# The sample attention's cache rows on SyncE's queue, loaded ahead as one stream

## The chip, the core and the metric

The kernel runs on one core of one Trainium2 chip. The metric is device time in microseconds of one execution. Three runs of the kernel before took 2106.47 to 2107.64 us, median 2107.42 us. One further execution was profiled; its trace spans 2100.4 us from the first to the last instruction.

Engine names are those of the profile: PE (TensorE's matrix products) and PEld (its weight loads), DVE (VectorE), ACT (ScalarE), POOL (GpSimd), and SP (SyncE), which here does nothing but issue DMAs. All DMAs, whoever issues them, are carried by the core's 16 DMA engines. L1062 is line 1062 of the kernel that the row belongs to.

## The reference, cut to what matters

One decoder layer runs for 256 prompt tokens and for 8 sample sequences of 4 tokens each (288 columns together). The part that the change touches is the sample tokens' attention over cached keys and values, in three groups of heads with different strides:

```python
DIL_GROUPS = ((128, 1), (512, 4), (2048, 16))

def _dilated_group(q, k, v, q_idx, dil, n_back):
    dist = jnp.arange(n_back + 1) * dil
    idx = q_idx[:, None] - dist[None, :]
    valid = idx >= 0
    idx = jnp.maximum(idx, 0)
    kg = k[:, idx].astype(jnp.float32)
    vg = v[:, idx].astype(jnp.float32)
    s = jnp.einsum('bqhd,bqjhd->bqhj', q.astype(jnp.float32), kg) * (HD_B ** -0.5)
    s = jnp.where(valid[None, :, None, :], s, -jnp.inf)
    m = jnp.max(s, axis=-1)
    p = jnp.exp(s - m[..., None])
    return jnp.einsum('bqhj,bqjhd->bqhd', p, vg), m, jnp.sum(p, axis=-1)
...
    h = _rms_norm(x, g_pre_mix)
    (qa, ka, va, za, ba, aa, qb, kb, vb, uc, ga, gb, gc) = _split(h @ w_in, IN_SPLITS)
...
    kv_all = [jnp.concatenate([win_hists[gi].astype(dt), kv_new[gi]], axis=1) for gi in range(N_GROUPS)]
```

Beside it stand a gated delta rule, a pooling branch, the prompt's own attention, a merge, and a feed-forward block. All weights are float32, 2048 wide, and each is read once.

## The kernel before, in words

**The weight stream.** Every projection is a list of weight tiles `raw` of 256 rows by 512 columns (512 KB). `load` issues the tile's DMA on SyncE's queue into one of five buffers. `feed` splits it: ACT casts it to `wh` (L180), and DVE subtracts to get the remainder `wl` (L184); each has three buffers. PE then runs 24 matmuls of 128x288 for the tile (L229 to L231): `wh` with the high part of the activations, `wh` with the low part, `wl` with the high part. A tile's third matmul therefore waits for DVE.

**Background work.** After each tile `step` advances a few generators by a rate. `attn_sample` is one of them: about 3.65 of its steps per tile, one DVE instruction each. The order of all instructions on an engine is fixed when the kernel is built, by a scheduler with a simulated timeline, and each engine executes its own in that order.

**The sample attention.** Two passes over 59 rows each, first over the keys, then over the values. A *row* is a tile `kr` of 128 partitions by 512 numbers (256 KB). In each pass, in this order: 32 rows of group 1 and 16 rows of group 2 from the caches `cache_win2` and `cache_win3` (L1062), two rows of this step's own keys or values, each loaded by four DMAs of 64 KB from a DRAM scratch `scr` (L1043), eight rows of group 0 from `cache_win1` (L1071), and one more from the scratch (L1074). A row of groups 1 and 2 is used by four DVE instructions, one per head; a row of group 0 by sixteen. In the first pass they write `junk` and a score (L1083), in the second they accumulate into `ot` or `big` (L1130, L1132). Between the passes come the maxima and exponentials. Each DVE instruction of the passes waits for the one before it (`chain`).

**Where a row's 128 partitions come from.** For groups 1 and 2 the cached tokens are taken apart as `(q m r)`, and one row takes four neighbouring tokens `r` of each of 32 blocks:

```python
src = cw[g].rearrange("b (q m r) k h d -> m k r (b q) (h d)", q=4, r=dil)
dq.dma_start(kr, src[m, kv][:4])
```

So the DMA's source is 4 by 32 by 512 numbers, outermost size 4, with 2 KB in one piece. Rows of group 0 have a source of 128 by 512, as the weight tiles have 128 outermost.

**Queues.** `dq` is GpSimd's queue. On it stand, in the scheduler's order, the row loads, POOL's own arithmetic for the delta rule and the pooling branch, and stores of states and of new keys and values (`win_prompt`, `scr`, `win_sample`, `gdn_prompt`, `gdn_sample`). There are five `kr` buffers; a load waits until DVE has used up the row that was in its buffer, and whatever stands behind it on POOL waits too. On SyncE's queue stand the weight tiles, the delta rule's states and small transposes, and later copies of the caches.

Of the kernel before, what the change touches and what calls it, by code (L numbers as in the profile page):

```python
# [9 lines left out]
F32 = mybir.dt.float32  # L10
# [4 lines left out]
PSUM = bass.MemoryType.PSUM  # L15
DRAM = bass.MemoryType.DRAM
# [6 lines left out]
TAIL = 'eveqqqeeeqqqevqe'  # L23
PM_POOL = (5, 7, 9, 11, 13, 15)
PCB = 3
SQP = (1, 3, 5, 7, 9, 11, 13)
EPS = 1e-6
SC = 128.0 ** -0.5
# [61 lines left out]
class Layer:  # L90
# [3 lines left out]
    def __init__(self, ctx, tc, a, o):  # L94
        self.ctx, self.tc, self.nc, self.a, self.o = ctx, tc, tc.nc, a, o
        P = self.pool
        self.cp = P("cp")
        self.raw_p = P("rawp", 5)
        self.wh_p = P("whp", 3)
        self.wl_p = P("wlp", 3)  # L100
        self.up = P("up")
        self.sm = P("sm", 2)
        self.dr = P("dr", space=DRAM)
        self.pm = P("pm", 4, space=PSUM)
        self.pb = P("pb", 4, space=PSUM)
        self.ufree = deque(range(NU))
        self.uslot = {}
        self.bg = []
        self.chained = {}
        self.tiles = deque()  # L110
        self.pend = deque()
        self.items = []
        self.n = 0
        self.raws = deque()
        self.hold = None
        self.out_a, self.out_b, self.out_c = {}, {}, {}
        self.dq = self.nc.gpsimd
# [1 line left out]
    def pool(self, name, bufs=1, **k):  # L119
        return self.ctx.enter_context(self.tc.tile_pool(name=name, bufs=bufs, **k))  # L120

# [1 line left out]
    def U(self, cols=NT, dt=F32, name="u"):  # L123
        s = self.ufree.popleft()
        self.n += 1
# [28 lines left out]
            off += w  # L154
        return d

# [1 line left out]
    def load(self):  # L158
        nc, parts = self.nc, self.tiles.popleft()
        left = len(self.tiles)  # L160
# [81 lines left out]
        return ins  # L242

    def chain(self, ins, key="sample"):
        """Each of these instructions waits for the one before: what the projections need gets between them."""
        if key in self.chained:
            self.behind(ins, self.chained[key])
        self.chained[key] = ins
# [18 lines left out]
        self.bg.append(g)  # L267
        return g

# [1 line left out]
    def cache_copies(self):  # L271
        """Chunks of the window caches' kept rows, copied in DRAM between the weight tiles."""
        for g in (2, 1, 0):
            keep = (124, 508, 1024)[g]
            src, dst = self.a[f"cache_win{g + 1}"][0], self.o[f"win{g + 1}_sample"][0]
            r0 = src.shape[1] - keep
            step = (124, 127, 128)[g]
            for b in range(8):
                for r in range(0, keep, step):
                    yield dst[b, r:r + step], src[b, r0 + r:r0 + r + step]  # L280
# [33 lines left out]
        self.free(t)  # L314

    def warm_sqrt(self, src):
        """Has the square root's table loaded ahead of its use."""
        self.nc.scalar.activation(self.small(1, "warm"), src[:, 0:1], AF.Sqrt)

    def rms_rows(self, *accs):  # L320
        """1 / rms of the tokens, along the free dimension of all partitions (in PSUM)."""
        nc, st = self.nc, (0, 128, 160)
        p = self.ps("rms")
        for k, acc in enumerate(accs):
            for i, t in enumerate(st):
                nc.tensor.matmul(p[:, i:i + 1], lhsT=acc[:, t:t + 128], rhs=self.c["ones"][:, 0:1],
                                 start=k == i == 0, stop=k == len(accs) - 1, skip_group_check=True)
        r = self.small(3, "rs")
        nc.scalar.activation(r, p[:, 0:3], AF.Sqrt, bias=self.eps, scale=1.0 / D)
        nc.vector.reciprocal(r, r)  # L330
        p = self.ps("rmsb")
        for i, t in enumerate(st):
            nc.tensor.transpose(p[:, t:t + 128], r[:, i:i + 1].to_broadcast([128, 128]), self.c["ident"])
        return p[:, :NT]
# [11 lines left out]
            self.xT.append(x)  # L346

    def pre_norm(self, n):
        """x times the gain, split: the first projections run on it, and their outputs take the rows' rms."""
        for d in range(len(self.h0), n):  # L350
            self.h0.append(self.scaled_split(self.xT[d], self.p["g_pre_mix"][:, d:d + 1], "h0"))

# [110 lines left out]
            nc.scalar.activation(t2, pe[:, hg * 32:hg * 32 + 32], AF.Exp)  # L463
            self.egls.append(t2)

# [1 line left out]
    def mixer_plan(self):  # L467
        w = self.a["w_in"][0]
        H = lambda: self.h
# [76 lines left out]
        self.nc.gpsimd.dma_start(self.o["cstate"], self.cstate.rearrange("p a b -> p (a b)"))  # L546
        self.pa.__exit__(None, None, None)

# [1 line left out]
    def gdn_setup(self):  # L550
        nc, p = self.nc, self.pap
        self.pads = []
# [62 lines left out]
    def gdn(self, hg):  # L615
# [36 lines left out]
        for x in X9:  # L652
# [17 lines left out]
            if x < 8:  # L670
                t = self.U(name="lt4")
# [7 lines left out]
        nc.sync.dma_start(dlt.rearrange("x p i -> p x i"), ltc)  # L679
        lb = pp.tile([32, 32, 32], F32, name="lb")  # L680
        nc.sync.dma_start(lb.rearrange("p j i -> p (j i)"), dlt.rearrange("x (b j) i -> (x b) (j i)", b=4))
        # sample tokens
        for _ in self.gdn_sample(hg, G, LA[8], kn[4], bv[4], beta, egc, nbe, kdc, qsc):
            yield
        self.free(LA.pop(8), kn.pop(), bv.pop(), G["kqs"])
# [121 lines left out]
    def gdn_sample(self, hg, G, la, kn, bv, beta, egc, nbe, kdc, qsc):  # L807
# [55 lines left out]
        nc.vector.tensor_tensor(so, so, qsc[:, X:X + 1], op=OP.mult)  # L863
        nc.scalar.activation(o[:, 0:128], o[:, 0:128], AF.Copy, scale=so)
        yield
        # state update: block (l, b) of the masked outer products
        kd = kn[:, 0:128]
        nc.gpsimd.tensor_scalar(kd, kd, kdc[:, X:X + 1], None, op0=OP.mult)
        vz = [self.U(name="vz") for _ in range(4)]
# [35 lines left out]
        G["os"] = o  # L905
        yield

# [1 line left out]
    def evac_qkv(self, kind, g):  # L909
        vT = []  # L910

        def evac(h, ps):
            nc = self.nc
            t = self.res.popleft()
            nc.scalar.copy(t, ps)
            if kind == 2:
                vT.append(t)
            else:
                (self.kT if kind == 1 else self.qT)[g, h] = t
            if h < 3:  # L920
                return
            src = vT if kind == 2 else [(self.kT if kind == 1 else self.qT)[g, j] for j in range(4)]
            for tb in ([2] if kind == 0 else [1, 2] if (kind == 1 and g == 0) else [0, 1, 2]):
                w = NS if tb == 2 else 128
                p = self.ps("knat")
                for j in range(4):
                    nc.tensor.transpose(p[:w, j * 128:j * 128 + 128], src[j][:, tb * 128:tb * 128 + w],
                                        self.c["ident"])
                for hp in range(2):
                    n = self.U(name="nat")  # L930
                    cs = slice(hp * 256, hp * 256 + 256)
                    if hp == 0:
                        nc.scalar.copy(n[:w, :256], p[:w, cs])
                    else:
                        nc.vector.tensor_copy(n[:w, :256], p[:w, cs])
                    if tb < 2:
                        if not (g == 0 and tb == 0):
                            o = self.o[f"win{g + 1}_prompt"][0, 0].rearrange("r k h d -> r k (h d)")
                            r0 = 0 if g == 0 else tb * 128
                            self.dq.dma_start(o[r0:r0 + 128, kind - 1, cs], n[:, :256])  # L940
                    else:
                        self.dq.dma_start(self.scr[kind, g][:, cs], n[:NS, :256])
                        if kind > 0:
                            o = self.o[f"win{g + 1}_sample"][0].rearrange("b r k h d -> b r k (h d)")
                            self.dq.dma_start(o[:, WIN[g] - 4:, kind - 1, cs], n[:NS, :256])
                    if kind == 2 and tb < 2:
                        self.vn[g, tb, hp] = n
                    else:
                        self.free(n)
            self.free(*vT)  # L950
        evac.res = 4
        return evac

# [77 lines left out]
    def attn_sample(self, pool):  # L1031
# [8 lines left out]
        def by_t(dst, kind, g):  # L1040
            src = scr[kind, g].rearrange("(b t) d -> t b d", t=4)
            for t in range(4):
                dq.dma_start(dst[t * 32:t * 32 + 32], src[t][:, None, :].to_broadcast([8, 4, 512]))  # L1043
# [7 lines left out]

        cw = [a["cache_win1"][0], a["cache_win2"][0], a["cache_win3"][0]]

        def row():
            return pool.tile([128, 512], F32, name="kr", bufs=5)

        def rows(kv):
            for g, dil, n in ((1, 4, 32), (2, 16, 16)):
                src = cw[g].rearrange("b (q m r) k h d -> m k r (b q) (h d)", q=4, r=dil)
                for m in range(n):  # L1060
                    kr = row()
                    dq.dma_start(kr, src[m, kv][:4])  # L1062
                    yield g, (m if g == 1 else 32 + m), kr
            for g in (1, 2):
                kr = row()
                by_t(kr, 1 + kv, g)
                yield g, 47 + g, kr
            src = cw[0].rearrange("b (s m) k h d -> m k (b s) (h d)", m=8)
            for m in range(8):
                kr = row()  # L1070
                dq.dma_start(kr, src[m, kv])  # L1071
                yield 0, m, kr
            kr = row()
            dq.dma_start(kr, scr[1 + kv, 0][:, None, :].to_broadcast([32, 4, 512]))  # L1074
            yield 0, 8, kr

        for g, m, kr in rows(0):
            for h in range(4):
# [75 lines left out]
            nc.vector.tensor_copy(self.ob[h][:, NP:], p[:, h * 32:h * 32 + 32])  # L1154
        yield

# [1 line left out]
    def pool_open(self):  # L1158
        self.drain(self.attn_p)
        self.pc = self.tc.tile_pool(name="pc", bufs=PCB, side="right", reuse_waits="tile")  # L1160
# [66 lines left out]
        for k in range(4):  # L1227
            self.free(*self.pooled[gp * 4 + k])

# [1 line left out]
    def evac_gate(self, n):  # L1231
        def evac(b, ps):
            t = self.res.popleft()
# [89 lines left out]
        nc.scalar.copy(self.r2, self.rms_rows(acc))  # L1323
        self.free(acc)

# [1 line left out]
    def evac_ffn_gate(self, f):  # L1327
        def evac(b, ps):
            self.drain(self.ffn_rms)
# [134 lines left out]
```

## Time and profile before

| what | us |
|---|---|
| runs (three) | 2106.47 to 2107.64, median 2107.42 |
| span of the profiled execution | 2100.4 |
| DVE busy in the span | 1320.4 |
| ACT busy | 886.4 |
| POOL busy | 340.2 |
| rows used in the first pass, from the first to the last start (L1083) | 419.9 to 666.3 |
| rows used in the second pass (L1130, L1132) | 688.4 to 974.6 |

The profile's page gives a total for the profiled execution only as its span; 2107.42 less 2100.4 leaves 7.0 us that lie around the span. Times within the trace are counted from the span's start. A view by windows gives, for a stretch of time, each engine's busy time with its number of instructions, then the mean granted TensorE clock (1.00 is full), the mean busy share of the 16 DMA engines, and GB/s. The DMA share can exceed 1, since packets on one engine overlap a little. In the DMA view a queue's share is the time that its packets took, as a share of 16 engines over the stretch; q1 is SyncE's queue and q0 GpSimd's.

### The profile page before, as it was taken

Reading aid. Unit: us, or ns where it says so; the run is one execution under the profiler, and the core shown is the slowest. Engines: PE = TensorE matmul, PEld = TensorE weight load, DVE = VectorE, ACT = ScalarE, POOL = GpSimd, SP = SyncE. Lnnn points to the kernel's source line nnn. Section 1 sums busy time; section 2 is a strip of 40 time slices with the busy share of each in tenths; the row PEclk is TensorE's granted clock in tenths of the full one; section 3 lists DMA queues with packets and bytes.
Section 4 is the critical chain, followed back from the end, with each engine's and each line's share of the span. In section 5 each row is a group of like instructions: output and inputs, shape, how many; then the busy total and the mean of one; then the engine's idle time right before and its main releaser. Section 6 shows DMA issues by size and latency. Waiting matters only on the chain. (4 is left out here: it accounts for less than half of the span.)

```text
span 2100.4 us, 38731 instructions
## 1 busy us (share of the span) xinstructions
PE 2026.7 (96%) x15218; PEld 1996.9 (95%) x15218; DVE 1320.4 (63%) x2829; ACT 886.4 (42%) x1402; POOL 340.2 (16%) x570
## 2 busy tenths in 40 slices
PE   8999899989899998999999989999999999999998
PEld 7999798979899898999999989999999999999997
DVE  7979557577787788997347475543455445544455
ACT  4654374343354333433334453343334333333344
POOL 4426403543311222201000030000000000000001
PEclk9999999999999999999999999999999999999999
DMA  6565446899965899765577746767776767776762
GB/s 233 156 192 180 132 145 190 215 210 235 235 184 157 190 215 232 222 186 161 161 257 225 224 142 221 225 218 229 224 229 213 227 215 226 221 228 217 225 208 97
DMA packets 229048, 425.50 MB, mean 203 GB/s; under 512 B 42738, under 2 KB 66818, under 8 KB 227202
## 3 DMA queue, kind: packets, MB, share of 16 engines
q1 hardware_dynamic: 194912, 380.52, 60.8%
q0 software_dynamic: 33808, 41.92, 8.3%
q8 instruction: 119, 1.95, 0.4%
q10 hardware_dynamic: 144, 0.59, 0.1%
q14 instruction: 65, 0.52, 0.1%
HBM read 410.44 MB, written 66.63 MB: 227 GB/s over the span
## 5 line engine op out<-in xcount | busy, mean ns | idle before, releaser
L184 DVE TENSOR_TENSOR wl<-raw,wh 128x1024 fp32r<-128x1024 f32 x585 | 721.5, 1234 | 545.0 <-ACT wh L180 541.3
L180 ACT CAST wh<-raw 128x1024 fp32r<-128x1024 f32 x585 | 612.6, 1049 | 923.0 <-PE m L230 842.3
L229 PE MATMUL m<-hh,wh 128*128 128x288 f32 x1792 | 537.3, 302 | 10.2 <-DVE xp L1175 5.5
L231 PE MATMUL m<-hh,wl 128*128 128x288 f32 x1792 | 527.6, 300 | 13.5 <-DVE wl L184 13.5
L230 PE MATMUL m<-hl,wh 128*128 128x288 f32 x1792 | 534.0, 299 | 0.0
L229 PE MATMUL m<-xgh,wh 128*128 128x288 f32 x1408 | 414.7, 296 | 3.4 <-DVE fg L1331 1.8
L231 PE MATMUL m<-xgh,wl 128*128 128x288 f32 x1408 | 414.8, 296 | 2.5 <-DVE wl L184 2.5
L230 PE MATMUL m<-xgl,wh 128*128 128x288 f32 x1408 | 415.5, 296 | 1.0 <-DVE xgl L339 0.9
L231 PEld LDWEIGHTS m<-hh,wl 128*128 128x128 f32 x1792 | 338.5, 191 | 17.9 <-DVE wl L184 15.9
L229 PEld LDWEIGHTS m<-hh,wh 128*128 128x128 f32 x1792 | 341.7, 191 | 14.5 <-DVE xp L1175 6.0
L230 PEld LDWEIGHTS m<-hl,wh 128*128 128x128 f32 x1792 | 341.9, 191 | 1.3 <-issue 1.2
L229 PEld LDWEIGHTS m<-xgh,wh 128*128 128x128 f32 x1408 | 265.5, 189 | 4.3 <-DVE fg L1331 2.3
L230 PEld LDWEIGHTS m<-xgl,wh 128*128 128x128 f32 x1408 | 266.6, 189 | 2.1 <-DVE xgl L339 2.0
L231 PEld LDWEIGHTS m<-xgh,wl 128*128 128x128 f32 x1408 | 265.5, 189 | 3.0 <-DVE wl L184 3.0
L230 PE MATMUL m<-hidl,wh 128*128 128x288 f32 x704 | 207.5, 295 | 0.0
L229 PE MATMUL m<-hidh,wh 128*128 128x288 f32 x704 | 207.1, 294 | 0.0
L231 PE MATMUL m<-hidh,wl 128*128 128x288 f32 x704 | 206.5, 295 | 0.0
L1392 POOL TENSOR_TENSOR yo<-y,xr 128x288 f32<-128x288 f32 x7 | 5.6, 829 | 828.9 <-DVE y L1383 828.9
L230 PEld LDWEIGHTS m<-hidl,wh 128*128 128x128 f32 x704 | 132.4, 188 | 0.0
L229 PEld LDWEIGHTS m<-hidh,wh 128*128 128x128 f32 x704 | 132.2, 188 | 0.0
L231 PEld LDWEIGHTS m<-hidh,wl 128*128 128x128 f32 x704 | 132.1, 188 | 0.0
L1062 POOL DMA_DIRECT2D kr<-cache_win x96 | 65.6, 685 | 198.3 <-DVE junk L1083 80.1
(389 smaller groups left out, 2766.0 us busy)
## 6 DMA issues: line engine op xcount, KB each, us to landing
raw<-w_in SPq DMA_DIRECT2D x247, 512.0 KB, 4.3
raw<-w_gu SPq DMA_DIRECT2D x176, 512.0 KB, 4.0
raw<-w_down SPq DMA_DIRECT2D x88, 512.0 KB, 5.0
win_sample<-cache_win SPq DMA_DIRECT2D x64, 512.0 KB, 5.3
kr<-cache_win POOLq DMA_DIRECT2D x112, 256.0 KB, 10.6
raw<-w_out SPq DMA_DIRECT2D x32, 512.0 KB, 4.5
win_sample<-cache_win SPq DMA_DIRECT2D x32, 508.0 KB, 5.4
st<-state_gdn SPq DMA_DIRECT2D x64, 128.0 KB, 3.2
```

What stands on the lines that cost most here:

```text
L180: i = nc.scalar.copy(wh, raw)
L184: self.last_wl = nc.vector.tensor_tensor(wl, raw, wh.bitcast(F32), op=OP.subtract)
L229: nc.tensor.matmul(out, lhsT=wh[:, kk, c], rhs=xh, start=k == 0, stop=False)
L230: nc.tensor.matmul(out, lhsT=wh[:, kk, c], rhs=xl, start=False, stop=False)
L231: nc.tensor.matmul(out, lhsT=wl[:, kk, c], rhs=xh, start=False, stop=k == 2 * nk - 1)
L1062: dq.dma_start(kr, src[m, kv][:4])
L1392: (nc.vector if how == "v" else nc.gpsimd).tensor_tensor(out[:, d % 2], y, x, op=OP.add)
```

## The change

The rows of both passes become one list. A generator `ahead` keeps up to six rows loaded or under way and hands out the oldest; a row is handed out when the passes ask for it, so five more are on their way at that moment. The loads go out on SyncE's queue, and there are six `kr` buffers. A row that comes from the scratch still takes four DMAs where it did. `self.values` holds back the loads of the second list's later groups until the last value projection has been written to the scratch. What is computed, and the DVE instructions of the passes, stay as they were.

```diff
+KR = 6
...
+        self.values = False
...
             self.free(*vT)
+            self.values = self.values or (kind == 2 and g == 2)
...
-        def row():
-            return pool.tile([128, 512], F32, name="kr", bufs=5)
-
-        def rows(kv):
+        sq = nc.sync
+
+        def load(src, cached):
+            kr = pool.tile([128, 512], F32, name="kr", bufs=KR)
+            if cached:
+                sq.dma_start(kr, src)
+            else:
+                for t in range(4):
+                    sq.dma_start(kr[t * 32:t * 32 + 32], src[t][:, None, :].to_broadcast([8, 4, 512]))
+            return kr
+
+        def sources(kv):
+
             for g, dil, n in ((1, 4, 32), (2, 16, 16)):
                 src = cw[g].rearrange("b (q m r) k h d -> m k r (b q) (h d)", q=4, r=dil)
                 for m in range(n):
-                    kr = row()
-                    dq.dma_start(kr, src[m, kv][:4])
-                    yield g, (m if g == 1 else 32 + m), kr
+                    yield g, (m if g == 1 else 32 + m), src[m, kv][:4], True
             for g in (1, 2):
-                kr = row()
-                by_t(kr, 1 + kv, g)
-                yield g, 47 + g, kr
+                yield g, 47 + g, scr[1 + kv, g].rearrange("(b t) d -> t b d", t=4), False
             src = cw[0].rearrange("b (s m) k h d -> m k (b s) (h d)", m=8)
             for m in range(8):
-                kr = row()
-                dq.dma_start(kr, src[m, kv])
-                yield 0, m, kr
-            kr = row()
-            dq.dma_start(kr, scr[1 + kv, 0][:, None, :].to_broadcast([32, 4, 512]))
-            yield 0, 8, kr
+                yield 0, m, src[m, kv], True
+            yield 0, 8, scr[1 + kv, 0][:, None, :].to_broadcast([32, 4, 512]), True
+
+        def ahead():
+
+            todo = deque((kv,) + r for kv in range(2) for r in sources(kv))
+            got = deque()
+            while todo or got:
+                while todo and len(got) < KR:
+                    if todo[0][0] and not self.values:
+                        break
+                    kv, g, m, src, cached = todo.popleft()
+                    got.append((kv, g, m, load(src, cached)))
+                yield got.popleft()
+
+        stream = ahead()
+
+        def rows(kv):
+            for _ in range(59):
+                r = next(stream)
+                assert r[0] == kv
+                yield r[1:]
```

How this moves instructions on two engines, in the order in which each engine executes them. First SyncE's queue, from the delta rule's last small transpose (`dc`) on, where the first pass begins. Before:

```order
L704 DMA dc<-dx_4950 128x8x32 x2
L169 DMA raw<-w_in 128x2x512 x48
L169 DMA raw<-w_br_a 128x2x512 x4
L169 DMA raw<-w_in 128x2x512 x8
L169 DMA raw<-w_br_a 128x2x512 x4
```

And with the change, at the same place (its lines stand up to two lower in the file):

```order
L706 DMA dc<-dx_4950 128x8x32 x2
L171 DMA raw<-w_in 128x2x512 x4
L1062 DMA kr<-cache_win 128x1x512 x6
L171 DMA raw<-w_in 128x2x512 x3
L1062 DMA kr<-cache_win 128x1x512 x2
L171 DMA raw<-w_in 128x2x512
L1062 DMA kr<-cache_win 128x1x512 x2
L171 DMA raw<-w_in 128x2x512
L1062 DMA kr<-cache_win 128x1x512
L171 DMA raw<-w_in 128x2x512
```

The row loads now stand between the weight tiles' loads, first six in a row and then one or two behind each tile, in both passes.

Then GpSimd, at the same place of the program: the queries' loads (`qt`, `big`), the delta rule's arithmetic (`e`, `la`) and stores (`scr`, `win_prompt`, `win_sample`, `gdn_prompt`). Before:

```order
L1049 DMA big<-scr 128x1x512 x4
L1062 DMA kr<-cache_win 128x1x512 x5
L714 TENSOR_TENSOR e_539_5137<-la_4057,cc 128x128
L942 DMA scr<-nat_5038 32x256
L942 DMA scr<-nat_5041 32x256
L1062 DMA kr<-cache_win 128x1x512
L721 TENSOR_TENSOR la_4057<-la_4057,cc 128x128
L1062 DMA kr<-cache_win 128x1x512
L1043 DMA qt<-scr 32x1x512 x4
L1062 DMA kr<-cache_win 128x1x512 x11
L940 DMA win_prompt<-nat_5459 128x256
```

And with the change:

```order
L1052 DMA big<-scr 128x1x512 x4
L716 TENSOR_TENSOR e_539_5137<-la_4057,cc 128x128
L944 DMA scr<-nat_5038 32x256
L944 DMA scr<-nat_5041 32x256
L723 TENSOR_TENSOR la_4057<-la_4057,cc 128x128
L1046 DMA qt<-scr 32x1x512 x4
L942 DMA win_prompt<-nat_5459 128x256
```

GpSimd's rows are the same without the row loads. On PE, ACT and DVE the change moves a few neighbours past each other, mostly DVE's row instructions against its `wl`, and takes away or adds none.

## The prediction

> **What bounds the kernel now.** I read the page's busy shares first, then the windows of the two stretches in which row loads are dense, then who waits there, then the DMA view.
>
> ```profile
> span 2100.4 us, 38731 instructions
> PE 2026.7 (96%) x15218; PEld 1996.9 (95%) x15218; DVE 1320.4 (63%) x2829; ACT 886.4 (42%) x1402; POOL 340.2 (16%) x570
> ```
>
> PE is busy for all but 74 us, so only PE's idle time and its slow clock can be won, while anything that keeps weight tiles from it costs in full. The windows say where the change acts:
>
> ```profile
> core 0: us, PE busy (x) PEld busy (x) DVE busy (x) ACT busy (x) POOL busy (x), PEclk, DMA share, GB/s
> 410.00:560.00 150.00, 130.87 (x952) 128.17 (x950) 99.93 (x456) 57.79 (x114) 55.20 (x90) 0.95 0.99 221
> 700.00:850.00 150.00, 138.44 (x1000) 136.24 (x1000) 121.79 (x278) 53.16 (x70) 38.93 (x76) 0.97 1.03 222
> 1000.00:1050.00 50.00, 50.00 (x380) 50.00 (x380) 20.40 (x18) 19.67 (x24) 0.00 (x0) 1.00 0.55 160
> ```
>
> The first two are the stretches of groups 1 and 2, call them A (keys) and B (values). PE idles 19.1 us in A and 11.6 us in B, and the clock is below 1, while after the attention (1000 to 1050) PE never idles. The DMA engines are full in A and B (0.99, 1.03) at 221 and 222 GB/s. DVE's and PE's waits from 400 to 880 us (us in total, times, longest):
>
> ```profile
> DVE junk L1083 <- DMA kr<-cache_win: 43.8, 17, 8.5
> DVE ot L1132 <- DMA kr<-cache_win: 22.9, 15, 5.0
> PE m L231 <- DVE wl L184: 14.0, 7, 5.8
> ```
>
> The longest gap, in the timeline (start, duration, and the idle time before with what ended it), DVE first:
>
> ```profile
> 555.43 0.08 DVE L1083 DVE_READ_ACCUMULATOR junk<-kr,qt 128x1 f32 x1
> 560.12 0.29 DVE L1083 SCALAR_TENSOR_TENSOR junk<-kr,qt 128x128 f32<-128x128 f32 x1 [4.61 <-DMA kr<-cache_win]
> 560.34 1.22 DVE L184 TENSOR_TENSOR wl<-raw,wh 128x1024 fp32r<-128x1024 f32 x1
> ...
> 561.62 0.61 PE L231 MATMUL m<-hh,wl 128*128 128x288 f32 x1 [5.80 <-DVE wl L184]
> ```
>
> DVE stands 4.61 us before a late row, the remainder `wl` stands behind that row in DVE's fixed order, and PE waits 5.80 us for `wl`. Late rows are what stops PE. The question is what makes a row late, the issue on GpSimd or the transfer, and whether SyncE's queue changes that.
>
> **What GpSimd's queue costs.** Groups and waits of the tile `kr` in A (the second line: time that POOL's later loads stood for a row before):
>
> ```profile
> L1062 POOL DMA_DIRECT2D kr<-cache_win x44: 677/679/716, 412.7 to 546.4; - x44
> POOL kr L1062 <- DVE junk L1083: 43.3, 19, 7.5
> DMA to landing us min/median/max: 5.9/10.6/15.6
> ```
>
> A load occupies POOL 0.68 us (44 of them 30 us of 150) and mostly waits for a buffer that DVE empties: the scheduler already runs loads ahead as far as five buffers allow. Moving them frees POOL, which bounds nothing here (55.20 us busy in A), and the sixth buffer adds one row of lead. A row lands 10.6 us after its issue, so the transfer is what is slow.
>
> **What a row is to the DMA engines.** Between the passes there is a moment with one row load and nothing else: the window, and the same moment's queue line (packets, MB, share of 16 engines).
>
> ```profile
> 691.70:694.70 3.00, 3.00 (x24) 2.81 (x23) 2.88 (x7) 2.53 (x4) 0.00 (x0) 1.00 0.24 75
> q0 software_dynamic: 78, 0.23, 24.5%
> ```
>
> 24.5% of 16 is four: a row with a source of outermost size 4 uses 4 of the 16 DMA engines, 64 KB (65.5 thousand bytes) each, at 75 / (0.24 x 16) = 19.5 GB/s per engine. Now A and B in full (queue lines, then issues with their count and size):
>
> ```profile
> q1 hardware_dynamic: 8643, 16.66, 49.1%
> q0 software_dynamic: 15110, 16.31, 49.0%
> ...
> raw<-w_in SPq DMA_DIRECT2D x31, 512.0 KB, 9.9
> kr<-cache_win POOLq DMA_DIRECT2D x44, 256.0 KB, 9.9
> ```
>
> ```profile
> q1 hardware_dynamic: 11779, 21.66, 65.4%
> q0 software_dynamic: 11295, 11.42, 36.9%
> ...
> raw<-w_in SPq DMA_DIRECT2D x32, 512.0 KB, 11.6
> kr<-cache_win POOLq DMA_DIRECT2D x40, 256.0 KB, 12.6
> raw<-w_br_a SPq DMA_DIRECT2D x5, 512.0 KB, 10.6
> raw<-w_pool SPq DMA_DIRECT2D x4, 256.0 KB, 4.5
> ```
>
> In A GpSimd's queue fills 49.0% of the engines, twice what four can. So different rows on that queue sit on different fours, and the load spreads over all sixteen. No load on SyncE's queue before has an outermost size below 16, so no row shows which four it would use there. That is the open point on which everything hangs.
>
> **The sum if SyncE's queue always takes the same four** (my forecast). Then those four carry every row, plus a sixteenth of all else (32.8 thousand bytes per weight tile). At 19.5 GB/s a row takes 65.5 / 19.5 = 3.36 us and a tile 1.68 us on each of them.
> - A: 44 rows 147.8; 31 tiles 52.1; the rest of q0, 16.31 less 44 x 0.262 = 4.78 MB, over 16 engines, 15.3. Together 215 in place of 150 us: +65.
> - B: 40 rows 134.4; 32 + 5 + 4 half tiles = 39 tiles 65.5; 0.93 MB 3.0. Together 203: +53.
> - Slack: five tiles of lead can be used up in each stretch (8.4 us) and the sixth buffer brings one row (3.36): -24 for both. The 12 rows of groups 1 and 2 outside the stretches are loaded where DMA has room, as before.
> - POOL's freed issues and the DVE order: 0. They lie beside a longer wait; without that cover they are the gain of the first rival.
>
> Sum: +94 on the profiled execution, 2100.4 span and 7.0 around it, so 2107.4 + 94 = 2201; the execution stands at the median of the runs by that count. I say **2200**.
>
> The per-engine rate is the unknown price. Its ends: the weights alone in one microsecond, 356 / (0.95 x 16) = 23.4, and A itself, 221 / (0.99 x 16) = 14.0.
>
> ```profile
> 1010.00:1011.00 1.00, 1.00 (x10) 1.00 (x9) 0.86 (x1) 0.10 (x1) 0.00 (x0) 1.00 0.95 356
> ```
>
> At 23.4 A takes 179, B 169, less 20 of slack: +28, 2135. At 14.0 they take 300 and 283, less 33: +250, 2357. I take the row load alone, since four busy engines are that case, and lean below the top because weights mix in. So this case has its own range, 2135 to 2320.
>
> The Trainium skill, "DMA: Bandwidth & Descriptors", section "Why a DMA increments its semaphore by 16 and not by 1", says that a DMA runs on the largest count up to 16 that divides the outermost sizes of both sides, on the sync queue on the lowest-numbered engines, on GpSimd's on consecutive ones from a moving cursor. The trace agrees with the count (24.5%) and with the moving (49.0%); no run here shows SyncE's side. By that rule this case holds.
>
> **Rivals.**
> - *SyncE's queue spreads the rows.* The engines share the load as now. What can be won is PE's idle time in A and B, 19.1 + 11.6, and the slow clock, 0.05 x 150 + 0.03 x 150 = 12: at most 43 us, to 2064. For it: POOL's issue is gone, and one more row leads. Against: the engines are already full at 221 GB/s, so at the same rate the same bytes take the same time. Half of the bound: 2086.
> - *Spread, and nothing changes.* If 221 GB/s is what this mix of reads gives, the rows are as late as before, less one row of lead. 2107. The same page, section "Issuing engines are not separate DMA queues", says that queues share the 16 engines and that another issuer saves only issue time; by that the sum would be 0.
> - *Spread, but SyncE blocks.* A row load waits for its buffer until DVE has used a row, and weight tiles now stand behind it on SyncE; they wait themselves for a buffer that `wl` frees. With five tiles of lead this decides only when the row load waits longer than about four tiles, 4 x 24 / 7.6 = 12.6 us (380 matmuls in 50 us). DVE's longest wait of 8.5 us is below it; two such waits in one stretch would cost some 5 us each: 2117. Behind SyncE's waiting load also stands `poolh`, on which the pooling branch waits.
>
> That the change does not do what it says is excluded by the order: the loads stand on SyncE's queue, six ahead.
>
> **Chances.** Same four 0.70: SyncE's weight loads all cover the sixteen alike, nothing in the trace shows its queue moving on from one load to the next, and a load cut in four most plainly starts where all start. Spread and faster 0.16; spread and the same 0.09; blocking 0.05. The likeliest time is 2200. The range takes the first case from the cheap end to 2300 and, on the other side, the same, the blocking and the weaker part of the gain: 2090 to 2300. A measurement of this kernel can tell about 0.2% (4 us) from no change: slower 0.75, same 0.09, faster 0.16.
>
> **What would show it.** Right: in A and B of the new trace a DMA share well below 1 with landings of rows and tiles longer than now; DVE waiting on `kr` far above 67 us in total, PE on `wl`; a stretch of only row loads showing a share of about 0.25 however many are under way; POOL without row waits. Wrong: a DMA share near 1 in A and B, or shorter landings of `kr`; then the rows are spread, and the time falls or stays. If the four are fixed but the sum is off, the per-engine rate in A (GB/s over sixteen times the share) says by how much.

## The result, and the profile after

| kernel | median us | runs | ratio to before (95% interval) |
|---|---|---|---|
| before | 2106.94 | 2101.92 to 2107.64 (4) | |
| with the change | 2180.31 | 2178.31 to 2184.15 (4) | 1.0362 (1.0344 to 1.0380) |

The change makes the kernel 73.4 us slower. The profiled execution took 2178.31 us. Its page, in the lines that answer to those of before, begins with the span and the busy time of each engine:

```profile
span 2176.5 us, 38746 instructions
PE 2056.5 (94%) x15218; PEld 2020.6 (93%) x15218; DVE 1320.5 (61%) x2829; ACT 884.4 (41%) x1402; POOL 256.9 (12%) x440
```

The span grew by 76.1 us. PE runs the same 15218 matmuls in 29.8 us more (2056.5 against 2026.7), which goes with a lower granted clock (0.971 against 0.984 on the mean), and idles 46.3 us more (120.0 of the span against 73.7). DVE's and ACT's work is unchanged, and POOL has 83 us less of it. In the page's 40 slices of 54 us PE's holes stand from the eighth to the eleventh and from the fifteenth to the seventeenth, where the rows of groups 1 and 2 are loaded, with the DMA engines half to three quarters busy there:

```profile
PE   8998999878799977899999998999999999999998
DMA  7566356755575555665557774766676777767663
```

The rows of groups 1 and 2 now take longer to be used up. In the view of the tile `kr` the first pass (durations min/median/max in ns, then the first and the last start in us) reads, before and then after:

```profile
L1083 DVE SCALAR_TENSOR_TENSOR junk<-kr,qt x200: 253/291/296, 419.9 to 568.4; 128x128 f32<-128x128 f32 x100
```

```profile
L1107 DVE SCALAR_TENSOR_TENSOR junk<-kr,qt x200: 268/291/296, 411.8 to 609.0; 128x128 f32<-128x128 f32 x100
L1154 DVE TENSOR_SCALAR ot<-kr,sct x4: 275/279/285, 726.1 to 729.1; 128x128 f32<-128x128 f32 x4
L1156 DVE SCALAR_TENSOR_TENSOR ot<-kr,sct,ot x196: 334/352/405, 730.3 to 944.8; 128x128 f32<-128x128 f32 x196
```

So the keys' stretch, from the first to the last use, went from 148.5 to 197.2 us, and the values' (726.1 to 944.8) from 182.1 (688.4 to 870.5 before) to 218.7: +49 and +37. The windows of the two stretches, with the columns that the prediction's first table has:

```profile
410.00:600.00 190.00, 147.37 (x918) 140.86 (x917) 101.87 (x467) 51.54 (x104) 20.61 (x38) 0.85 0.54 166
760.00:930.00 170.00, 137.40 (x903) 133.17 (x902) 109.21 (x248) 44.97 (x57) 12.12 (x31) 0.89 0.60 180
```

Where the DMA engines were full before (0.99 at 221 GB/s), they now look half idle (0.54 at 166 GB/s), and yet everything waits for them. PE idles 42.6 us of the first stretch at a clock of 0.85. The waits from 400 to 960 us say for what (us in total, times, longest):

```profile
ACT wh L182 <- DMA raw<-w_in: 139.6, 34, 14.5
...
DVE junk L1107 <- DMA kr<-cache_win: 75.3, 38, 4.1
DVE wl L186 <- ACT wh L182: 60.9, 37, 6.4
...
PE m L233 <- DVE wl L186: 19.4, 16, 3.5
DVE ot L1156 <- DMA kr<-cache_win: 17.9, 13, 3.8
```

DVE waits 93 us for rows in place of 67. The largest wait is new in its size: ACT waits 139.6 us for weight tiles, where it waited 10.3 us before. Both kinds of load are late now.

The key to it is a moment in which little but rows is under way, here from 488 to 501 us: first the window, then the queue and the issues in it.

```profile
488.00:501.00 13.00, 8.01 (x56) 7.78 (x55) 5.75 (x30) 5.74 (x13) 0.33 (x1) 0.84 0.27 100
```

```profile
q1 hardware_dynamic: 632, 1.25, 25.5%
...
kr<-cache_win SPq DMA_DIRECT2D x5, 256.0 KB
```

Five row loads are issued in those 13 us, and SyncE's queue still keeps 25.5% of the sixteen engines busy, which is four. On GpSimd's queue the same kind of load had filled 49.0% before. SyncE's own timeline at this place (start, duration of the issues):

```profile
481.45 2.78 SPq L171 DMA_DIRECT2D raw<-w_in  x1
484.32 13.34 SPq L1062 DMA_DIRECT2D kr<-cache_win  x6
500.16 2.36 SPq L171 DMA_DIRECT2D raw<-w_in  x1
```

For some 16 us, from the end of one weight tile's issue to the start of the next, SyncE issues nothing but rows, and its six issues take 13.34 us of it. In the stretch from 420 to 600 us a weight tile's issue takes 2.9 us in the median, against 0.37 us before:

```profile
L169 SPq DMA_DIRECT2D raw<-w_in x41: 367/368/368, 421.4 to 592.7; - x41
```

```profile
L171 SPq DMA_DIRECT2D raw<-w_in x28: 391/2872/4729, 418.9 to 592.1; - x28
L1062 SPq DMA_DIRECT2D kr<-cache_win x42: 546/1372/4571, 423.4 to 583.9; - x42
```

Three theories can explain this much.

- **Theory 1, the same four engines.** Every row of groups 1 and 2 goes to the same four engines on SyncE's queue. Those four are the bound, and SyncE's slow issues follow from it: the four are behind, and the queue takes no more.
- **Theory 2, SyncE's order.** Rows and tiles share one in-order queue; a row load that waits for its buffer holds up the tiles behind it. How many engines a row uses does not matter.
- **Theory 3, the pieces.** A row is 128 pieces of 2 KB from far-apart addresses, which is slow to issue or to fetch on SyncE's queue, whatever engines carry it.

### The profile page after: what moved, and what is told of

It is laid out like the page before. It is cut to its first block, busy times and chain, and to the rows that moved or that the text cites. A ratio compares the mean times of both kernels' runs of the same rounds, so it can differ in the third digit from the quotient of the medians.

```text
span 2176.5 us, 38746 instructions
## 1 busy us (share of the span) xinstructions
PE 2056.5 (94%) x15218; PEld 2020.6 (93%) x15218; DVE 1320.5 (61%) x2829; ACT 884.4 (41%) x1402; POOL 256.9 (12%) x440
## 5 line engine op out<-in xcount | busy, mean ns | idle before, releaser
L231 PE MATMUL m<-hh,wh 128*128 128x288 f32 x1792 | 547.1, 307 | 22.9 <-DVE xp L1199 9.9
L233 PE MATMUL m<-hh,wl 128*128 128x288 f32 x1792 | 537.1, 306 | 19.1 <-DVE wl L186 18.9
L232 PE MATMUL m<-hl,wh 128*128 128x288 f32 x1792 | 543.0, 304 | 0.0
L231 PEld LDWEIGHTS m<-hh,wh 128*128 128x128 f32 x1792 | 350.3, 196 | 28.2 <-DVE xp L1199 10.3
L233 PEld LDWEIGHTS m<-hh,wl 128*128 128x128 f32 x1792 | 346.4, 195 | 26.2 <-DVE wl L186 24.2
L232 PEld LDWEIGHTS m<-hl,wh 128*128 128x128 f32 x1792 | 350.5, 196 | 1.3 <-issue 1.2
L1107 DVE SCALAR_TENSOR_TENSOR junk<-kr,qt 128x128 f32<-128x128 f32 x200 | 57.8, 289 | 87.9 <-DMA kr<-cache_win 75.3
```

Source lines behind the costliest of these rows:

```text
L231: nc.tensor.matmul(out, lhsT=wh[:, kk, c], rhs=xh, start=k == 0, stop=False)
L232: nc.tensor.matmul(out, lhsT=wh[:, kk, c], rhs=xl, start=False, stop=False)
L233: nc.tensor.matmul(out, lhsT=wl[:, kk, c], rhs=xh, start=False, stop=k == 2 * nk - 1)
L1107: self.chain(nc.vector.scalar_tensor_tensor(junk, kr[:, hs], SC, q, op0=OP.mult, op1=OP.mult, accum_out=out))
```

## The experiments

The first three keep the change and its instructions, in the same order on every engine, and alter only the source's outermost size. Ratios are to runs of the kernel before beside them: 2104.74 us median of 8 for the first four experiments, 2104.68 us of 7 for the others.

**32 outermost.** The same pieces and bytes per row, with the 32 blocks ahead of the 4 neighbours:

```diff
-                src = cw[g].rearrange("b (q m r) k h d -> m k r (b q) (h d)", q=4, r=dil)
+                src = cw[g].rearrange("b (q m r) k h d -> m k (b q) r (h d)", q=4, r=dil)
-                    yield g, (m if g == 1 else 32 + m), src[m, kv][:4], True
+                    yield g, (m if g == 1 else 32 + m), src[m, kv][:, :4], True
```

> Only the order of a row's 128 source pieces is changed (32 blocks outermost, 4 tokens inside), so a row's partitions stand in another order than the queries and the sample scores belong to other tokens; every instruction stands where it stands in the changed kernel, and the same bytes are read in the same 2 KB pieces. Theory 1 (the four engines): a row now spreads over 16 engines, the hot four are gone, 2065 to 2110, likeliest 2090. Theory 2 (SyncE's order: weight tiles stand behind row loads that wait for a buffer): order and waits are the same, 2180 as the changed kernel. Theory 3 (making a row's 128 pieces costs SyncE 1 to 3 us each): as many pieces, 2180.

Measured: 2052.47 us (2050.84 to 2060.28, 4 runs), ratio 0.9738 (0.9697 to 0.9778). Windows of the stretches that the prediction calls A and B, and the issue of a row, which took up to 8.45 us with the change:

```profile
410.00:560.00 150.00, 148.15 (x1143) 147.10 (x1142) 126.17 (x566) 67.41 (x129) 29.20 (x54) 1.00 0.87 272
700.00:850.00 150.00, 148.45 (x1116) 147.68 (x1115) 137.21 (x309) 61.04 (x79) 14.90 (x32) 1.00 0.73 233
...
L1062 SPq DMA_DIRECT2D kr<-cache_win x112: 328/540/1357, 406.7 to 849.5; - x112
```

PE is busy for 148 of 150 us at full clock, and 272 GB/s move at a share of 0.87. SyncE's order is untouched, and the pieces are the same but for their order within a load, so theory 2 falls, and theory 3 as far as the number and size of the pieces go; the run with four DMAs a row, below, keeps the order of their addresses too. The waits that theory 2 names have not even become shorter. SyncE's row loads wait as long for buffers from 400 to 960 us, first with the change, then with 32 outermost:

```profile
SPq L1062 <- DVE junk L1107: 46.4, 36, 3.2
SPq L1062 <- DVE ot L1156: 34.3, 26, 4.4
```

```profile
SPq L1062 <- DVE junk L1107: 40.4, 47, 3.2
SPq L1062 <- DVE ot L1156: 40.1, 42, 2.8
```

The slow issues are gone. The time lies below the expected 2065 to 2110: the gain over the kernel before, 52 us, was expected smaller.

**2 outermost.** The other way: rows on two engines, if theory 1 holds.

```diff
-                src = cw[g].rearrange("b (q m r) k h d -> m k r (b q) (h d)", q=4, r=dil)
+                src = cw[g].rearrange("b (q m r) k h d -> m k r (b q) (h d)", q=8, r=dil)
-                    yield g, (m if g == 1 else 32 + m), src[m, kv][:4], True
+                    yield g, (m if g == 1 else 32 + m), src[m % (n // 2), kv][:2], True
```

> Rows of groups 1 and 2 are read with outermost size 2 (2 neighbouring tokens of 64 blocks; other cached tokens than the computation needs, 256 KB in 2 KB pieces as before); every instruction stands where it stands in the changed kernel. Theory 1: a row falls on two engines, 131 thousand bytes each, 6.7 us at 19.5 GB/s; 48 rows and the tiles' share take about 390 us in the first pass against 197 measured with four, 405 against 219 in the second: about 2555, and a DMA share near 0.3 in both stretches. Theories 2 and 3: 2180.

Measured: 2390.37 us (one run). A stretch of only rows, and A:

```profile
538.00:554.00 16.00, 3.90 (x22) 3.67 (x21) 6.05 (x30) 1.42 (x2) 0.54 (x1) 0.61 0.13 50
...
410.00:560.00 150.00, 78.27 (x430) 72.92 (x429) 52.35 (x255) 27.78 (x69) 10.94 (x20) 0.74 0.29 94
```

(With this edit each cached piece is read for two of the rows.) A share of 0.13 is two of sixteen, and 50 GB/s are half of the 100 that four engines moved. Direction and mechanism are as theory 1 has them. The size was expected too large, because the expectation used the prediction's 19.5 GB/s per engine. From 430 to 700 us the two engines carried more, if they were busy throughout: 42 rows of 0.262 MB, halved, 5.5 MB each, and a sixteenth of the remaining 14.6 MB of q1 and of 2.36 MB of q0, together 6.6 MB in 270 us, about 24.3 GB/s.

```profile
q1 hardware_dynamic: 13041, 25.62, 29.1%
q0 software_dynamic: 1216, 2.36, 2.6%
...
L1062 SPq DMA_DIRECT2D kr<-cache_win x42: 520/1230/7130, 434.3 to 692.5; - x42
```

**8 outermost.** Between the two:

```diff
-                src = cw[g].rearrange("b (q m r) k h d -> m k r (b q) (h d)", q=4, r=dil)
+                src = cw[g].rearrange("b (q m r) k h d -> m k r (b q) (h d)", q=2, r=max(dil, 8))
-                    yield g, (m if g == 1 else 32 + m), src[m, kv][:4], True
+                    yield g, (m if g == 1 else 32 + m), src[m, kv][:8], True
```

> Rows of groups 1 and 2 are read with outermost size 8 (8 neighbouring tokens of 16 blocks; other cached tokens than the computation needs, same bytes and pieces); every instruction stands where it stands in the changed kernel. Theory 1: eight engines, a row 1.68 us on each; 44 rows 74, 31 tiles 52, the rest 15, together 141 of the 150 us of the first stretch, so PE sets the time again: 2085 to 2120. Theories 2 and 3: 2180.

Measured: 2088.21 us (2082.44 to 2092.29, 5 runs), ratio 0.9912 (0.9878 to 0.9946). A, DVE's wait for the keys' rows, and SyncE's queue from 470.5 to 475.5 us, where only row loads are issued:

```profile
410.00:560.00 150.00, 135.22 (x984) 131.05 (x983) 106.68 (x494) 57.88 (x117) 20.57 (x38) 0.97 0.79 227
...
DVE junk L1107 <- DMA kr<-cache_win: 34.1, 26, 3.7
...
q1 hardware_dynamic: 482, 0.93, 50.4%
```

A share of 50.4% is eight of sixteen. With 2, 4, 8 and 32 outermost the kernel takes 2390, 2180, 2088 and 2052 us. That ladder is what theory 1 says and neither of the others. Why 8 outermost are still 36 us above 32 was not tried apart; ACT still waits 56.7 us for weight tiles there.

**The queue alone.** The kernel before, five buffers and loads at their use; only the row loads stand on SyncE's queue.

```diff
-                    dq.dma_start(kr, src[m, kv][:4])
+                    nc.sync.dma_start(kr, src[m, kv][:4])
...
-                by_t(kr, 1 + kv, g)
+                by_t(kr, 1 + kv, g, nc.sync)
...
-                dq.dma_start(kr, src[m, kv])
+                nc.sync.dma_start(kr, src[m, kv])
...
-            dq.dma_start(kr, scr[1 + kv, 0][:, None, :].to_broadcast([32, 4, 512]))
+            nc.sync.dma_start(kr, scr[1 + kv, 0][:, None, :].to_broadcast([32, 4, 512]))
```

> The kernel before with its row loads on SyncE's queue, and nothing else: rows at their use, five buffers. Theory 1: the queue alone brings the cost, 2175 to 2200 (one row less of lead than the changed kernel). Theory 2: about the same, since the loads stand in the same queue. A theory 4, that the stream and the other order of DVE cost the time: 2107 or less.

Measured: 2178.82 us (2177.64 to 2180.53), ratio 1.0341 (1.0304 to 1.0377). A, and DVE's waits:

```profile
410.00:560.00 150.00, 113.25 (x739) 107.91 (x737) 79.48 (x373) 43.89 (x93) 17.32 (x32) 0.87 0.55 167
...
DVE junk L1083 <- DMA kr<-cache_win: 86.9, 44, 4.8
```

Time, share and GB/s are those of the whole change within a few parts in a hundred (0.53 and 165 GB/s in the same stretch): the queue brings all of the cost. The scheduler moves DVE's instructions here too, so this run alone does not clear their order; the first experiment does, which has the change's order throughout and is fast.

**The stream alone.** The change with its list, its five rows of lead and its six buffers, but on GpSimd's queue.

```diff
-        sq = nc.sync
+        sq = nc.gpsimd
```

> The changed kernel with the row stream on GpSimd's queue: six buffers and the list as changed, only the queue undone. Theory 1: the fours move again, so the cost is gone, 2095 to 2108. If the list or the sixth buffer had cost the time: 2180.

Measured: 2089.26 us (2085.98 to 2090.29), ratio 0.9926 (0.9903 to 0.9949). That is 15 us faster than before, a little below what was expected. DVE's wait for the values' rows fell from 22.9 us to 10.5, and the keys' stayed at 43.4 (43.8 before). These waits, and the windows of A and B:

```profile
DVE junk L1107 <- DMA kr<-cache_win: 43.4, 17, 9.8
DVE ot L1156 <- DMA kr<-cache_win: 10.5, 7, 4.3
...
410.00:560.00 150.00, 131.52 (x937) 128.00 (x936) 98.83 (x459) 56.75 (x111) 55.72 (x92) 0.94 0.98 218
700.00:850.00 150.00, 144.99 (x1080) 142.96 (x1080) 130.35 (x296) 58.59 (x79) 40.96 (x82) 1.00 1.03 241
```

In A the engines are as full as before at the same rate, and nothing is won. The gain is mostly in B. (On this queue the scheduler also orders DVE's instructions otherwise, so the 15 us are those of stream, buffer and order together.)

**Is GpSimd's queue held back too?** The kernel before with 32 outermost, on GpSimd's queue at its use:

```diff
-                src = cw[g].rearrange("b (q m r) k h d -> m k r (b q) (h d)", q=4, r=dil)
+                src = cw[g].rearrange("b (q m r) k h d -> m k (b q) r (h d)", q=4, r=dil)
-                    dq.dma_start(kr, src[m, kv][:4])
+                    dq.dma_start(kr, src[m, kv][:, :4])
```

> The kernel before (GpSimd's queue, rows at their use, five buffers) with only the order of a row's source pieces changed, 32 blocks outermost; the partitions' order no longer fits the queries, as in the run of the changed kernel. It asks where the 55 us below the kernel before came from in that run. If four engines a row cost time on GpSimd's queue too: 2050 to 2075. If it is GpSimd's queue itself (two queues sharing the engines, 0.68 us of POOL per load): 2095 to 2108.

Measured: 2054.49 us (2052.59 to 2055.88), ratio 0.9766 (0.9739 to 0.9792), so about 50 us faster than before. A, with the landing times of `kr` there, which were 5.9/10.6/15.6 us before:

```profile
410.00:560.00 150.00, 148.25 (x1143) 147.19 (x1142) 129.24 (x573) 67.63 (x128) 58.64 (x109) 1.00 0.83 268
...
DMA to landing us min/median/max: 2.8/4.0/8.3
```

Loads of outermost size 4 cost the kernel before some 50 us as well, although they moved over all sixteen engines; no instruction changes its place on any engine between the two kernels. With 32 outermost the queue hardly matters: this interval and that of the last experiment below overlap.

**Four DMAs a row.** The row of the change cut into its four neighbours, each a DMA with 32 outermost, every partition where it was:

```diff
-                sq.dma_start(kr, src)
+                for r in range(4 if src.shape[0] == 4 else 0):
+                    sq.dma_start(kr[r * 32:r * 32 + 32], src[r])
+                if src.shape[0] != 4:
+                    sq.dma_start(kr, src)
```

> The changed kernel, with each row of groups 1 and 2 loaded by four DMAs of 32 partitions and outermost size 32, so all data in its right place. Theory 1: sixteen engines, 2050 to 2085, the upper part if four issues a row (0.33 to 0.55 us each, 1.3 to 2.2 us against a tile every 3 to 5 us) hold up SyncE. Theory 3 (pieces cost SyncE): 2180 or more.

Measured: 2068.40 us (2067.00 to 2069.66), ratio 0.9829 (0.9807 to 0.9852). A, and the issues of the rows:

```profile
410.00:560.00 150.00, 140.11 (x1022) 138.55 (x1021) 117.39 (x539) 59.63 (x117) 24.40 (x45) 0.94 0.82 245
...
L1063 SPq DMA_DIRECT2D kr<-cache_win x384: 310/419/1587, 398.2 to 795.3; - x192
```

Four issues of 0.42 us stand in place of one of 1.2 us, and the time still falls by 112 us. Each partition gets the same bytes from the same address as with the change; only the number of DMAs and the spread over the engines differ. With this the far-apart addresses of theory 3 can't be what costs these 112 us.

**One DMA a row, for use.** 32 outermost as in the first experiment, with the queries, the selection matrix, the mask and the maxima laid out for the new order of partitions (`t` fastest, then `b`); five of its edits:

```diff
-    d["sel1"] = (t // 32 == c % 4) & ((t % 32) // 4 == c // 4)
+    d["sel1"] = (t % 4 == c % 4) & (t // 16 == c // 4)
...
-    mt[:, 48:] = t % 4 == 0
+    mt[:, 48:] = t // 4 % 4 == 0
...
-            for t in range(4):
-                dq.dma_start(dst[t * 32:t * 32 + 32], src[t][:, None, :].to_broadcast([8, 4, 512]))
+            for b in range(8):
+                dq.dma_start(dst[b * 16:b * 16 + 16], src[b][None].to_broadcast([4, 4, 512]))
...
-                src = cw[g].rearrange("b (q m r) k h d -> m k r (b q) (h d)", q=4, r=dil)
+                src = cw[g].rearrange("b (q m r) k h d -> m k (b q) r (h d)", q=4, r=dil)
...
-        dq.dma_start(dmt.rearrange("c (q h) -> (c q) h", h=4), mt)
+        dtt = dmt.rearrange("(t b) (q h) -> b q t h", b=8, h=4)
+        for b in range(8):
+            dq.dma_start(dtt[b], mt[b * 16:b * 16 + 16])
```

> The changed kernel with 32 blocks outermost and one DMA a row, and the queries, masks, maxima and sums set to the new order of partitions, so all data in its right place; this step's own rows and the queries take eight small DMAs where they took four. Theory 1: as the run with the order alone, 2050 to 2070.

Measured: 2051.59 us (2050.85 to 2052.88), ratio 0.9750 (0.9728 to 0.9772). It beats both kernels. A and B:

```profile
410.00:560.00 150.00, 148.69 (x1149) 147.86 (x1147) 129.60 (x577) 68.46 (x129) 32.99 (x61) 1.00 0.85 266
700.00:850.00 150.00, 148.45 (x1117) 147.70 (x1116) 136.77 (x304) 60.85 (x80) 14.36 (x32) 1.00 0.73 235
```

What bounded A and B is gone: PE is busy for 148.7 and 148.5 of 150 us there.

## Why the prediction was right, and where its sum was off

**The mechanism.** The forecast was that SyncE's queue puts every row on the same four engines, and that these bound both stretches. The runs show it: a share of 25.5% with five rows issued, 0.13 with two outermost, 50.4% with eight, the ladder of times at an unchanged order of instructions, and the same loss from the queue alone. Which of the sixteen these four are, no run shows; that they also carry a sixteenth of the weights is an inference. Of the signs that were named, the low DMA share, the quarter in a stretch of rows and POOL without row waits came. DVE's waits for rows rose from 67 to 93 us, less than "far above", and PE's for `wl` from 14.0 to 19.4. The landings can't be read: the changed kernel's trace gives none for these loads.

The Trainium skill, "DMA: Bandwidth & Descriptors", section "Why a DMA increments its semaphore by 16 and not by 1", says that a DMA issued on the sync queue runs on the lowest-numbered engines, as many as the largest number up to 16 that divides the outermost sizes of both sides. The trace agrees with the counts of two, four and eight (13.1%, 25.5% and 50.4%) and with every row falling on the same ones; which numbers these engines have it does not show.

**The load term was 33 us too large.** It gave 65 and 53 us for the two stretches; the rows' spans grew by 49 and 37. The mis-sized part is the rate of one engine, 19.5 GB/s in the forecast. It came from the 3 us of a single row load; why a single load is slower than several in line, no run shows. Measured in the change's own stretches (queue lines from 420 to 600 us and from 760 to 930, and the rows of the second; those of the first, 42, are above):

```profile
q1 hardware_dynamic: 14114, 27.50, 49.5%
q0 software_dynamic: 1408, 2.63, 4.6%
```

```profile
q1 hardware_dynamic: 15929, 29.92, 58.6%
q0 software_dynamic: 160, 0.55, 0.9%
...
L1062 SPq DMA_DIRECT2D kr<-cache_win x34: 388/1306/3902, 761.2 to 924.7; - x34
```

Taken as busy throughout, one of the four carries a quarter of 42 rows, 2.75 MB, and a sixteenth of the other 16.5 and 2.63 MB, 1.20: together 3.95 MB in 180 us, 21.9 GB/s. In the second it is 2.23 and 1.34 MB in 170 us, 21.0 GB/s. With these rates the forecast's own bytes (4.20 and 3.96 MB for each of the four) take 192 and 188 us, +80 where the rows' spans grew by 85. Rows alone ran at 96 / (0.255 x 16) = 23.6 GB/s (q1's 1.25 MB in the 13 us from 488 to 501). The prediction's check, GB/s over sixteen times the share, was badly chosen: in the first stretch it gives 166 / (0.54 x 16) = 19.2, which is no rate of the four: it divides all bytes by all busy time, and about half of both lies on the other twelve.

**The slack term was 15 us too large.** Of 24 us that buffers were to give back, 9 came: 85 us longer stretches cost 76 us of span, and the first row's earlier start (411.8 in place of 419.9) makes up 8 of the 9. The weights' five tiles of lead gave nothing that the trace shows.

**The base was 5 us too high.** The 7.0 us around the span were the difference of two different executions. The changed kernel's profiled run is 2178.31 for a span of 2176.5, so 1.8 us lie around it, and the profiled execution of before took about 2102. Set right, the three give 2102.2 + 85 - 9 = 2178, the profiled run of the change. The three errors, 33 less 15 and 5 more, are the 23 us by which the forecast's 2201 lies above it: it was luck that the slack's error took back nearly half of the load's.

**The path to PE was only half named.** The forecast followed the wait over a late row, DVE and `wl`. The larger wait is ACT's for the tile itself, 139.6 us, with `wl` then waiting for `wh`. The forecast's sum had the tile's sixteenth on the loaded four, so that the size holds, and its signs named longer landings of tiles, but as waits only DVE's for rows and PE's for `wl`.

**The rivals.** "SyncE blocks" took the row loads' waits for buffers for a cause; they are there, some 80 us in the two passes, but with 32 outermost they are as long and cost nothing. "Spread and faster" described a world that the first experiment built: spread rows do bring a gain, 52 us there and 53 in the last experiment (2104.68 to 2051.59). That is more than the 43 that the rival allowed, because its bound counted only A and B of the profile before and left out the losses beside them: in the last experiment PE runs 314 more matmuls in A and B, 41 us at 380 in 50 us, and 43 more from 560 to 700 us (1068 against 1025), 6 us. "Spread, and nothing changes" holds for the choice of the queue once rows have 32 outermost (2051.6 and 2052.5 on SyncE's, 2054.5 on GpSimd's). The Trainium skill, "DMA: Bandwidth & Descriptors", section "Issuing engines are not separate DMA queues", says that another issuer saves issue time only. With 32 outermost the runs agree with it; for loads of outermost size 4 the measurement decides against it: the queue alone costs 3.41%.

**The freed POOL** was costed at 0, and nothing contradicts it. The stream with its sixth buffer is worth 15 us on GpSimd's queue, while on SyncE's, where the four engines bound, it changes nothing: 2178.82 without it, 2180.31 with it.

**What stays open.** Why the moving fours of the kernel before reached only 221 GB/s at a share of 0.99, where loads with 32 outermost reach 268 at 0.83, is not settled: by engine and busy time 14.0 against 20.2 GB/s. Not the rows alone are slower there: in the trace's packet records a packet of 2 KB on SyncE's queue takes 144 ns on the mean in A, against 105 with 32 outermost. Beside the count of engines two things differ between these runs, the packets, as the last section shows, and the order of a load's addresses (32 far-apart blocks for each neighbour, or four neighbours together); no run on GpSimd's queue separates them, as the four DMAs did on SyncE's. The 17 us between four DMAs a row and one may be the issues or that order of addresses, which also differs; neither was tried by itself.

## What to carry to other kernels

Before a load is moved to another queue, look at how many DMA engines one such load uses: a moment of only such loads shows it as a share of sixteen, and if that share is a quarter however many are under way, the few engines are the bound while the mean looks half idle. Write the access pattern so that one load spreads over all sixteen before choosing the queue (an outermost size of 32 here; 8 was still 36 us slower); here that was worth 50 us on the old queue and 128 us on the new one, and the choice of the queue then hardly anything. Take a per-engine rate from a stretch in which such loads follow each other, not from a single one: here they gave 23.6 and 19.5 GB/s.

## What the runs showed of the hardware that was not expected

- SyncE's issue of a load is not of fixed length. From 420 to 600 us a weight tile's issue took 0.37 us in the median before and with 32 outermost on SyncE's queue, although the engines were full before (a share of 0.99 in A). With the change, where every row falls on the same four, it took 2.9 us in the median (4.7 at most). So a load that uses all sixteen then stands behind loads that use four.
- On GpSimd's queue loads of outermost size 4 come with many packets under 512 bytes, and the same loads on SyncE's queue do not. The packets from 410 to 560 us, in the kernel before, with the change, and on GpSimd's queue with 32 outermost:

```profile
DMA packets 23767, 33.15 MB, mean 221 GB/s; under 512 B 11576, under 2 KB 11576, under 8 KB 23753
```

```profile
DMA packets 12706, 24.72 MB, mean 165 GB/s; under 512 B 1286, under 2 KB 1286, under 8 KB 12694
```

```profile
DMA packets 17995, 40.16 MB, mean 268 GB/s; under 512 B 2767, under 2 KB 2767, under 8 KB 17979
```

That is some 200 small packets for each of the 44 rows (11576 less 2767, over 44). In the trace's packet records 9510 of the 11576 have 8 bytes and take 12 ns each, 114 us of the 2400 that sixteen engines have in the stretch, so their own time is small. What they are, and whether they slow the other packets, was not tried; they may be part of why the kernel before moved 221 GB/s with full engines.
